# The last recurrent head of a hybrid layer takes two block sizes per step instead of one

## The chip, the cores and the metric

The kernel runs on one core of a Trainium2 chip. The metric is the device time of one execution in microseconds (us); for each kernel the median of several runs is given. A core has a matrix engine (PE, with its weight loads shown as PEld), a vector engine (DVE), a scalar engine (ACT), a general engine (POOL) and a sync engine (SP) that starts most transfers. Each works through its own list of instructions in order and waits for the others on semaphores. So a late instruction on one engine delays everything that stands behind it there, whether that needs the late data or not.

## The reference, cut to what matters

One layer of a model with 1024 tokens and width 1024, all in float32: a norm, one combined projection, then dilated attention (8 heads of 64) beside a gated linear recurrence (4 heads of 128), a projection of both, and a feed-forward part of width 4096. The change touches the recurrence alone. Within a chunk of 64 tokens it computes

```
diff = b[:, :, :, None, :] - b[:, :, None, :, :]      # b: running sum of the log gates
decay = jnp.exp(jnp.where(causal, diff, -jnp.inf))
a = jnp.einsum('bhtk,bhsk,bhtsk->bhts', qc, kc, decay)
o = o_inter + jnp.einsum('bhts,bhsv->bhtv', a, vc)
```

Here `a[t, s]` is the weight that token t gives to an earlier token s, with the product of all gates between them in it, separately for each of the 128 channels.

## The kernel before, in words

A float32 matmul of full precision is made here of three passes over high and low parts (`three_pass`, L91 to L93); a **group** below is three matmuls of 128x512, one for each pass. A weight tile comes by DMA, ACT rounds it to its high part (`wh`, L87) and DVE subtracts for the low part (`wl`, L88).

The recurrence uses chunks of 128 tokens, and `at` holds the weights `a` of all eight chunks. They are built up by block size. For blocks of c tokens, the queries of each second block and the keys of each first block are multiplied by their own gates inside the block (kept in `qt` and `kt`), a matmul gives all products of the two, a predicated copy under a mask writes those that belong to this size into `at`, and then `qt`, `kt` and the block totals `tot` are brought to size 2c. The diagonal comes from two sums over the channels (`pd`, L514), that go through a multiplication with the identity.

`hgrn_core` does this in two ways. Heads 0 to 2 climb two sizes per **step** (c to 4c, three steps, L542 to L574). Each 128x128 tile of keys is used as two halves of 64 columns, so that the array holds two chunk halves side by side, and the queries are first gathered into three sets of 32 columns by `quarter_sets` (L476; two ACT copies and two DVE products for each half of the tokens). A step is 16 matmuls of 64-column halves by 96 columns in two banks; behind it DVE runs products for `qt`, `kt` and `tot`, the products of the next `quarter_sets`, and six predicated copies. One last matmul of 64x64 blocks (L585) makes the size that is left. Head 3 instead takes one size per **level**, seven levels (L601 to L624): eight matmuls of 128x64 (L608; the trace counts each of these float32 matmuls twice), and on DVE a product for `kt` (L612), one for `qt` (L614), one for `tot` (L618) and one predicated copy under `masks` (L619).

Between steps and levels `fill(ns)` (L196) lets PE do other work: it pulls pieces from generators in `queue` until the given nominal time is used up, and what is overdrawn is carried on as a debt. A piece is mostly one group, counted as 650 ns. For heads 0 to 2 the pieces belong to the next recurrent head's projections. For head 3 they are `attn_proj` (L799), the projections of attention's first head pairs: queries in two halves (`pm_aq`, read by DVE into `qf`, L820, and split by ACT into `hiq`, L747, and by POOL, L748), values half 0 (`pm_av`, into `vf`, L837), keys half 0 and 1 (`pm_ak`, into `kf`, L754), values half 1. In the fourth piece of keys half 0 stand the transposes of `vf` (`values_turn`, L783, matmul L787, into the bank `pvt`). Generators that are not used up here are pulled on by the attention's steps later, the last of them at about 450 us.

Just ahead of head 3's core stands an exponential of one column (L1326), whose only purpose is to have ACT load its table of functions. The order of the instructions on each engine is that in which the code is written; buffers of the same name rotate.

Of the kernel before, what the change touches and what calls it, by code (L numbers as in the profile page):

```python
# [8 lines left out]
F32 = mybir.dt.float32  # L9
# [8 lines left out]
P = 128  # L18
# [19 lines left out]
def hymba_layer(ctx, tc, x, w_in, w_out, w_ff1, w_ff2, g_pre, lb_logits, g_mix, g_post,  # L38
# [28 lines left out]
    masks = cp.tile([P, len(LEVELS), 64], U8, name="masks")  # L67
# [313 lines left out]
    V.tensor_copy(masks, mraw)  # L381
# [123 lines left out]
    def hgrn_core(h, scale, after=None):  # L505
        hd = heads[h]
        inat, gate, prod, qt, kt, tot = (hd[n] for n in ("inat", "gate", "prod", "qt", "kt", "tot"))
        ready = quarter_sets(hd, h, 0, tot) if h < HH - 1 else None
        fill((5900 if 0 < h < HH - 1 else 5200) * scale)
        at = slab("S", f"at{h}", F32, (P, NT, P))  # L510
        for hf in range(2):
            pd = bank("pv", f"pd{h}_{hf}")
            for q in range(2):
                TE.matmul(pd, ones.to_broadcast([P, P]), prod[q][:, hf * 512:hf * 512 + 512], start=q == 0, stop=q == 1)  # L514
            pdv = pd.rearrange("p (n c) -> p n c", n=4)
            if h == HH - 1:
                V.tensor_tensor(out=at[:, hf * 4:hf * 4 + 4], in0=ident.unsqueeze(1).to_broadcast([P, 4, P]),
                                in1=pdv, op=ALU.mult)
                continue
            for a, b in halves:  # L520
                V.tensor_tensor(out=at[a:b, hf * 4:hf * 4 + 4, :64],
                                in0=ident[a:b, a:b].unsqueeze(1).to_broadcast([64, 4, 64]),
                                in1=pdv[a:b, :, a:b], op=ALU.mult)
# [5 lines left out]
        if h < HH - 1:  # L529
            fill(1200 * scale)  # L530
            totals = slab("P", f"tot{h}")
            for step in range(3):
                c = 4 ** step
                nb = 32 // c
                sets, cv = ready
                got = []
                for u in range(2):
                    pl = bank(("s", "t", "pv")[step], f"pl{h}_{step}{u}").rearrange("p (n q) -> p n q", n=4)
                    for n in range(4):
                        qs = sets[u][:, n].rearrange("p (s w) -> p s w", s=3)  # L540
                        for g, (a, b) in enumerate(halves):
                            TE.matmul(pl[a:b, n, :96], kt[:, (4 * u + n) * P + a:(4 * u + n) * P + b],  # L542
                                      qs[:, :, 32 * g:32 * g + 32], start=True, stop=True, skip_group_check=True)
                    got.append(pl)
                w = T // (4 * c)
                at_ = (0, 768, 960)[step]
                tots = totals[:, at_:at_ + 3 * w].rearrange("p (i w) -> p i w", i=3)
                u23, u123, nx = (tots[:, i] for i in range(3))
                cw = cv.rearrange("p n b f -> p (n b) f")
                q4 = qt.rearrange("p (m f c) -> p m f c", f=4, c=c)  # L550
                k4 = kt.rearrange("p (m f c) -> p m f c", f=4, c=c)

                def spread(ap, k=c):
                    return ap.unsqueeze(2).to_broadcast([P, w, k])
                V.tensor_tensor(out=q4[:, :, 1], in0=q4[:, :, 1], in1=spread(cw[:, :, 0]), op=ALU.mult)
                for hf in range(2):
                    n4 = slice(hf * 4, hf * 4 + 4)
                    V.tensor_tensor(out=qt[:, hf * 512:hf * 512 + 512].rearrange("p (n b f c) -> p n b (f c)", n=4, f=4, c=c)
                                    [:, :, :, 2 * c:],
                                    in0=sets[hf][:, :, 128:].rearrange("p n (b w) -> p n b w", b=nb),  # L560
                                    in1=cv[:, n4, :, 0:1].to_broadcast([P, 4, nb, 2 * c]), op=ALU.mult)
                V.tensor_tensor(out=u23, in0=cw[:, :, 2], in1=cw[:, :, 3], op=ALU.mult)
                V.tensor_tensor(out=u123, in0=cw[:, :, 1], in1=u23, op=ALU.mult)
                V.tensor_tensor(out=nx, in0=cw[:, :, 0], in1=u123, op=ALU.mult)
                if step < 2:
                    ready = quarter_sets(hd, h, step + 1, nx)
                V.tensor_tensor(out=k4[:, :, 2], in0=k4[:, :, 2], in1=spread(cw[:, :, 3]), op=ALU.mult)
                V.tensor_tensor(out=k4[:, :, 1], in0=k4[:, :, 1], in1=spread(u23), op=ALU.mult)
                V.tensor_tensor(out=k4[:, :, 0], in0=k4[:, :, 0], in1=spread(u123), op=ALU.mult)
                for u, pl in enumerate(got):  # L570
                    for part_, mask, c2 in ((0, own[:, 2 * step], c), (2, own[:, 2 * step + 1], 2 * c),
                                            (1, near[:, step], 2 * c)):
                        av = at[:, 4 * u:4 * u + 4, :64].rearrange("p n (b two c) -> p n b two c", two=2, c=c2)
                        V.copy_predicated(  # L574
                            av[:, :, :, 1, :],
                            mask.rearrange("p (b c) -> p b c", c=c2).unsqueeze(1).to_broadcast([P, 4, 32 // c2, c2]),
                            pl[:, :, part_ * 32:part_ * 32 + 32].rearrange("p n (b c) -> p n b c", c=c2))
                cur = nx
                table_part()
                fill(3500 * scale)  # L580
                table_part()
                fill(3500 * scale)
            pl = bank("s", f"pl{h}_6")
            for n in range(NT):
                TE.matmul(pl[:64, n * 64:(n + 1) * 64], kt[:, n * P:n * P + 64], qt[:, n * P + 64:(n + 1) * P],  # L585
                          start=True, stop=True)
            S.activation(at[64:, :, 64:], at[64:, :, :64], AF.Copy)
            G.memset(at[64:, :, :64], 0.0)
            S.activation(at[:64, :, 64:], pl[:64].rearrange("p (n c) -> p n c", n=NT), AF.Copy)
            kv, qv = (x.rearrange("p (n two c) -> p n two c", two=2, c=64) for x in (kt, qt))  # L590
            cv = cur.rearrange("p (n two) -> p n two", two=2)
            V.tensor_tensor(out=qv[:, :, 1], in0=qv[:, :, 1], in1=cv[:, :, 0:1].to_broadcast([P, NT, 64]), op=ALU.mult)
            V.tensor_tensor(out=kv[:, :, 0], in0=kv[:, :, 0], in1=cv[:, :, 1:2].to_broadcast([P, NT, 64]), op=ALU.mult)
            nx = tp.tile([P, NT], F32, tag="tot8", name=f"tot{h}_8", bufs=1)
            V.tensor_tensor(out=nx, in0=cv[:, :, 0], in1=cv[:, :, 1], op=ALU.mult)
            cur = nx
            fill(3400 * scale)
        else:
            cur = tot
            fill(1200 * scale)  # L600
            for li, c in enumerate(LEVELS):  # L601
                nb = 64 // c
                qv = qt.rearrange("p (b two c) -> p b two c", two=2, c=c)
                kv = kt.rearrange("p (b two c) -> p b two c", two=2, c=c)
                av = at.rearrange("p n (b two c) -> p n b two c", two=2, c=c)
                pl = bank("s", f"pl{h}_{li}")
                for n in range(NT):
                    TE.matmul(pl[:, n * 64:(n + 1) * 64], kt[:, n * P:(n + 1) * P],  # L608
                              qv[:, n * nb:(n + 1) * nb, 1, :], start=True, stop=True)
                w = T // (2 * c)  # L610
                cv = cur[:, :2 * w].rearrange("p (b two) -> p b two", two=2)
                V.tensor_tensor(out=kv[:, :, 0, :], in0=kv[:, :, 0, :],  # L612
                                in1=cv[:, :, 1:2].to_broadcast([P, w, c]), op=ALU.mult)
                V.tensor_tensor(out=qv[:, :, 1, :], in0=qv[:, :, 1, :],  # L614
                                in1=cv[:, :, 0:1].to_broadcast([P, w, c]), op=ALU.mult)
                nx = slab("P", f"tot{h}_{w}") if w > 32 else \
                    tp.tile([P, w], F32, tag=f"tot{w}", name=f"tot{h}_{w}", bufs=1)
                V.tensor_tensor(out=nx[:, :w], in0=cv[:, :, 0], in1=cv[:, :, 1], op=ALU.mult)  # L618
                V.copy_predicated(  # L619
                    av[:, :, :, 1, :],  # L620
                    masks[:, li].rearrange("p (b c) -> p b c", c=c).unsqueeze(1).to_broadcast([P, NT, nb, c]),
                    pl.rearrange("p (n b c) -> p n b c", n=NT, c=c))
                cur = nx
                fill((3700 if li == 0 else 2900 if li < 3 else 2200) * scale)  # L624
# [1701 lines left out]
```

## Time and profile before

| | us |
|---|---|
| three runs, median (lowest, highest) | 1198.26 (1198.24, 1198.39) |
| the profiled execution, its own time | 1197.81 |
| its span in the trace | 1195.6 |
| PE busy | 1186.2 (99% of the span) |
| DVE / ACT / POOL busy | 838.1 / 543.9 / 295.8 |

The profile is of one execution. Its page gives busy times and the chain of work that ended last; other views are the timeline (start, duration, engine, line, operation, output from inputs, how many alike in a row; in brackets the idle time ahead on that engine and what ended it), and windows (busy time per stretch, the granted clock of PE as a share of full speed, the share of DMA). Matmuls overlap, so that the time one takes from PE is read from start to start, not from its duration. Head 3's core lies at about 234 to 290 us.

### The profile page before, as it was taken

Reading aid. Unit: us, or ns where it says so; the run is one execution under the profiler, and the core shown is the slowest. Engines: PE = TensorE matmul, PEld = TensorE weight load, DVE = VectorE, ACT = ScalarE, POOL = GpSimd, SP = SyncE. Lnnn points to the kernel's source line nnn. Section 1 sums busy time; section 2 is a strip of 40 time slices with the busy share of each in tenths; the row PEclk is TensorE's granted clock in tenths of the full one; section 3 lists DMA queues with packets and bytes.
Section 4 is the critical chain, followed back from the end, with each engine's and each line's share of the span. In section 5 each row is a group of like instructions: output and inputs, shape, how many; then the busy total and the mean of one; then the engine's idle time right before and its main releaser. Section 6 shows DMA issues by size and latency. Waiting matters only on the chain.

```text
span 1195.6 us, 17551 instructions
## 1 busy us (share of the span) xinstructions
PE 1186.2 (99%) x6486; PEld 1014.5 (85%) x6486; DVE 838.1 (70%) x1393; ACT 543.9 (45%) x1068; POOL 295.8 (25%) x283
## 2 busy tenths in 40 slices
PE   9999999999999999999999999999999999999997
PEld 8898989888888888888888888888888888888886
DVE  5686969576666667675697666776687653578796
ACT  7633424322556667755653222222244544444562
POOL 0122222011111110152502777566540000000022
PEclk9999999999999999999999999999999999999999
DMA  5222323145454645362424465553687434533337
GB/s 220 71 68 85 98 84 98 52 119 144 125 133 104 153 135 143 96 233 96 169 97 161 174 215 207 179 183 142 218 325 273 159 105 143 174 89 105 106 106 282
DMA packets 90548, 175.48 MB, mean 147 GB/s; under 512 B 14944, under 2 KB 42464, under 8 KB 90464
## 3 DMA queue, kind: packets, MB, share of 16 engines
q1 hardware_dynamic: 90320, 174.37, 44.9%
q8 instruction: 51, 0.84, 0.3%
q14 instruction: 33, 0.27, 0.1%
q10 hardware_dynamic: 144, 0.00, 0.0%
HBM read 116.91 MB, written 47.99 MB: 138 GB/s over the span
## 4 chain that ended last, share of the span: by engine, by line
PE 96%; ACT 2%; DVE 1%; DMA 1%; issue 1%; POOL 0%; DVEq 0%; POOLq 0%; ACTq 0%
PE f L2066 18%; PE f2s L2066 7%; PE pig L91 3%; PE pig L93 2%; PE pig L92 2%; PE pwo L93 2%; PE pwo L91 2%; PE pwo L92 2%; PE pm_aq L91 1%; PE pm_f L91 1%; PE pm_ak L91 1%; PE pm_aq L93 1%; PE pm_aq L92 1%; PE pm_f L93 1%; PE pm_f L92 1%; PE pm_ak L93 1%
## 5 line engine op out<-in xcount | busy, mean ns | idle before, releaser
L88 DVE TENSOR_TENSOR al<-ar,ah 128x1024 fp32r<-128x1024 f32 x56 | 70.6, 1261 | 80.2 <-ACT ah L87 77.9
L2066 PE MATMUL f<-bh,ah 128*128 128x512 f32 x320 | 124.5, 389 | 0.0
L2066 PE MATMUL f<-bl,ah 128*128 128x512 f32 x320 | 124.5, 389 | 0.0
L2066 PE MATMUL f<-bh,al 128*128 128x512 f32 x320 | 124.5, 389 | 0.0
L87 ACT ACTIVATE ah<-ar 128x1024 fp32r<-128x1024 f32 x56 | 59.2, 1056 | 87.2 <-DMA ar<-actd 86.8
L2066 PEld LDWEIGHTS f<-bh,al 128*128 128x128 f32 x320 | 60.1, 188 | 12.6
L2066 PEld LDWEIGHTS f<-bl,ah 128*128 128x128 f32 x320 | 60.1, 188 | 12.5
L2066 PEld LDWEIGHTS f<-bh,ah 128*128 128x128 f32 x320 | 60.1, 188 | 12.3
L2140 POOL TENSOR_SCALAR lbl<-ssq 128x1 f32<-128x1 f32 x4 | 3.3, 821 | 245.7 <-ACT fd L2136 245.6
L1689 POOL TENSOR_TENSOR e<-x,e 128x512 f32<-128x512 f32 x14 | 21.6, 1540 | 130.1 <-DVE x L1640 123.0
L2066 PE MATMUL f2s<-bl,ah 128*128 128x512 f32 (+1 forms) x128 | 48.9, 382 | 0.0
L2066 PE MATMUL f2s<-bh,al 128*128 128x512 f32 (+1 forms) x128 | 48.9, 382 | 0.0
L2066 PE MATMUL f2s<-bh,ah 128*128 128x512 f32 (+1 forms) x128 | 48.9, 382 | 0.0
L732 POOL TENSOR_SCALAR tout<-traw 128x256 f32<-128x256 f32 x16 | 18.8, 1176 | 101.2 <-DMA traw<-in_bias_tab_dram 101.2
L88 DVE TENSOR_TENSOR bl<-br,bh 128x1024 fp32r<-128x1024 f32 x32 | 40.1, 1253 | 1.1 <-ACT bh L87 1.0
L2083 ACT ACTIVATE acc<-f 128x512 f32<-128x512 f32 x28 | 16.7, 597 | 48.6 <-PE f L2066 48.6
L87 ACT ACTIVATE bh<-br 128x1024 fp32r<-128x1024 f32 x32 | 33.6, 1051 | 4.3 <-PE f L2066 2.9
L88 DVE TENSOR_TENSOR wl<-raw,wh 128x1024 fp32r<-128x1024 f32 x21 | 25.9, 1234 | 10.2 <-ACT wh L87 10.2
L778 POOL TENSOR_TENSOR kl<-kf,kh 64x512 fp32r<-64x512 f32 x12 | 15.4, 1287 | 69.5 <-ACT kh L777 48.0
L91 PE MATMUL pwo<-woh,mt 128*128 128x512 f32 x80 | 32.2, 402 | 0.0
L93 PE MATMUL pwo<-woh,mt 128*128 128x512 f32 x80 | 31.3, 391 | 0.0
L92 PE MATMUL pwo<-wol,mt 128*128 128x512 f32 x80 | 31.2, 390 | 0.0
(1728 smaller groups left out, 3901.4 us busy)
## 6 DMA issues: line engine op xcount, KB each, us to landing
ar<-actd SPq DMA_DIRECT2D x56, 512.0 KB, 3.6
br<-in_w_ff_dram SPq DMA_DIRECT2D x16, 1024.0 KB, 5.8
raw<-in_w_in_dram SPq DMA_DIRECT2D x28, 512.0 KB, 4.2
w1r<-in_w_ff_dram SPq DMA_DIRECT2D x14, 1024.0 KB, 6.4
actd<-e SPq DMA_DIRECT2D x17, 768.0 KB, 4.3
actd<-e SPq DMA_DIRECT2D x11, 1024.0 KB, 4.1
xr<-in_x_dram SPq DMA_DIRECT2D x8, 512.0 KB, 8.2
raw<-in_w_out_dram SPq DMA_DIRECT2D x8, 512.0 KB, 3.6
```

Source lines behind the costliest of these rows:

```text
L87: S.activation(hi, src, AF.Copy)
L88: eng.tensor_tensor(out=lo, in0=src, in1=f32(hi), op=ALU.subtract)
L91: TE.matmul(dst, lhs[0], rhs[0], start=start, stop=False)
L92: TE.matmul(dst, lhs[0], rhs[1], start=False, stop=False)
L93: TE.matmul(dst, lhs[1], rhs[0], start=False, stop=stop)
L732: G.tensor_scalar(by_class(dst[:, part_ * w:(part_ + 1) * w]), in_blocks(raw[:, FAR * DIL:]), 8.0, None, op0=ALU.mult)
L778: G.tensor_tensor(out=kl[a:b], in0=src, in1=f32(kh[a:b]), op=ALU.subtract)
L1689: eng[0].tensor_tensor(out=e1[:, 3], in0=a21, in1=e1[:, 2], op=ALU.add)
L2066: TE.matmul(pm, a[:, j, c], b[:, j, d], start=start and j == 0 and q == 0, stop=stop and j == 1 and q == 2, skip_group_check=True)
L2083: S.activation(acc_at(p, i), pm, AF.Copy)
L2140: G.tensor_scalar(base[:, t:t + 1], sums[j][:, t:t + 1], 1.0 / D, EPS, op0=ALU.mult, op1=ALU.add)
```

## The change

Head 3 now runs the same three steps and the 64x64 matmul as the others. Its levels are gone from the code, and with them the tile `masks` and the cast that filled it (L381). The fillings in head 3 were scaled by 1.15 and are now scaled by 1.0; the first, ahead of `pd`, goes from 5980 to 5200 ns nominal, and that is from ten groups to eight. All line numbers of the changed kernel are lower, by 2 at L80 and by 34 at the end.

```diff
-    masks = cp.tile([P, len(LEVELS), 64], U8, name="masks")
...
-    V.tensor_copy(masks, mraw)
...
     def hgrn_core(h, scale, after=None):
         hd = heads[h]
         inat, gate, prod, qt, kt, tot = (hd[n] for n in ("inat", "gate", "prod", "qt", "kt", "tot"))
-        ready = quarter_sets(hd, h, 0, tot) if h < HH - 1 else None
+        ready = quarter_sets(hd, h, 0, tot)
         fill((5900 if 0 < h < HH - 1 else 5200) * scale)
...
-            if h == HH - 1:
-                V.tensor_tensor(out=at[:, hf * 4:hf * 4 + 4], in0=ident.unsqueeze(1).to_broadcast([P, 4, P]),
-                                in1=pdv, op=ALU.mult)
-                continue
             for a, b in halves:
                 V.tensor_tensor(out=at[a:b, hf * 4:hf * 4 + 4, :64],
                                 in0=ident[a:b, a:b].unsqueeze(1).to_broadcast([64, 4, 64]),
                                 in1=pdv[a:b, :, a:b], op=ALU.mult)
...
-        if h < HH - 1:
-            fill(1200 * scale)
-            totals = slab("P", f"tot{h}")
-            for step in range(3):
...
-            cur = nx
-            fill(3400 * scale)
-        else:
-            cur = tot
-            fill(1200 * scale)
-            for li, c in enumerate(LEVELS):
...
-                fill((3700 if li == 0 else 2900 if li < 3 else 2200) * scale)
+        fill(1200 * scale)
+        totals = slab("P", f"tot{h}")
+        for step in range(3):
...
+        cur = nx
+        fill(3400 * scale)
...
-        last_gate = hgrn_core(h, 1.15 if last else 1.0, open_attention if last else None)
+        last_gate = hgrn_core(h, 1.0, open_attention if last else None)
```

Three places show how the instructions now stand. A row is the line, the operation, the output with its buffer number, the inputs, and the shape.

The first is ACT at the start of head 3's core. Before:

```order
L463 ACTIVATE prh3_2602<-pr31_2735 128x512
L1326 ACT_TABLE_LOAD
L1326 ACTIVATE texp_2740<-nhalf_86 128x1
L87 ACTIVATE wh17_2758<-raw17_2513 128x1024
L473 ACTIVATE rc1_2767<-rrow_128 128x512
L474 ACTIVATE rrow_128<-rc1_2767 128x512
L747 ACTIVATE hiq00_2780<-qf00_2778 128x512
```

and in the change:

```order
L461 ACTIVATE prh3_2600<-pr31_2733 128x512
L1292 ACT_TABLE_LOAD
L1292 ACTIVATE texp_2738<-nhalf_85 128x1
L485 ACTIVATE qs3_00_2740<-qt3_2513 128x4x64
L489 ACTIVATE qs3_00_2740<-qt3_2513 128x4x32
L485 ACTIVATE qs3_01_2745<-qt3_2513 128x4x64
L489 ACTIVATE qs3_01_2745<-qt3_2513 128x4x32
L86 ACTIVATE wh17_2766<-raw17_2511 128x1024
L471 ACTIVATE rc1_2775<-rrow_127 128x512
L472 ACTIVATE rrow_127<-rc1_2775 128x512
L713 ACTIVATE hiq00_2788<-qf00_2786 128x512
```

The four gathering copies stand between the table load and the next weight's rounding, and so ahead of all that follows on ACT.

The second is DVE around the read of the values, `vf`. Before:

```order
L619 COPY_PREDICATED at3_2794<-masks_78,pl3_1_2854 128x256x2
L88 TENSOR_TENSOR wl18_2878<-raw18_2623,wh18_2877 128x1024
L612 TENSOR_TENSOR kt3_2604<-kt3_2604,tot3_256_2865 128x128x4
L614 TENSOR_TENSOR qt3_2515<-qt3_2515,tot3_256_2865 128x128x4
L618 TENSOR_TENSOR tot3_128_2900<-tot3_256_2865 128x128
L619 COPY_PREDICATED at3_2794<-masks_78,pl3_2_2889 128x128x4
L837 TENSOR_TENSOR vf00_2906<-pm_av00_2847,rrow_128 128x512
L791 TENSOR_TENSOR v0_2846<-pvt00_2925,v0_2846 128x8x64
```

and in the change:

```order
L560 TENSOR_TENSOR kt3_2602<-kt3_2602,tot3_2815 128x64x4
L561 TENSOR_TENSOR kt3_2602<-kt3_2602,tot3_2815 128x64x4
L562 TENSOR_TENSOR kt3_2602<-kt3_2602,tot3_2815 128x64x4
L567 COPY_PREDICATED at3_2795<-own_78,pl3_10_2909 128x4x8x4
L567 COPY_PREDICATED at3_2795<-own_78,pl3_10_2909 128x4x4x8
L567 COPY_PREDICATED at3_2795<-near_79,pl3_10_2909 128x4x4x8
L567 COPY_PREDICATED at3_2795<-own_78,pl3_11_2918 128x4x8x4
L567 COPY_PREDICATED at3_2795<-own_78,pl3_11_2918 128x4x4x8
L567 COPY_PREDICATED at3_2795<-near_79,pl3_11_2918 128x4x4x8
L803 TENSOR_TENSOR vf00_2961<-pm_av00_2887,rrow_127 128x512
L757 TENSOR_TENSOR v0_2886<-pvt00_2980,v0_2886 128x8x64
```

The read of the values stood behind the third level and stands now behind the whole second step (`pl3_10` and `pl3_11` are its two banks).

The third is PE around the transposes of `vf`. Before:

```order
L91 MATMUL pm_ak00_2912<-hTh00_90,wh18_2877 128x512
L92 MATMUL pm_ak00_2912<-hTl00_91,wh18_2877 128x512
L93 MATMUL pm_ak00_2912<-hTh00_90,wl18_2878 128x512
L787 MATMUL pvt00_2925<-ident_77,vf00_2906 128x128 x4
L608 MATMUL pl3_3_2936<-qt3_2515,kt3_2604 128x64 x8
L91 MATMUL pm_ak00_2912<-hTh10_92,wh18_2877 128x512
```

and in the change:

```order
L90 MATMUL pm_ak00_2967<-hTh00_89,wh18_2903 128x512
L91 MATMUL pm_ak00_2967<-hTl00_90,wh18_2903 128x512
L92 MATMUL pm_ak00_2967<-hTh00_89,wl18_2904 128x512
L753 MATMUL pvt00_2980<-ident_77,vf00_2961 128x128 x4
L90 MATMUL pm_ak00_2967<-hTh10_91,wh18_2903 128x512
L91 MATMUL pm_ak00_2967<-hTl10_92,wh18_2903 128x512
```

The transposes keep their place among the groups; three levels lay ahead of them and two steps do now, and the level that followed them at once is gone.

More of the change, by code (lines that the diff above doesn't have):

```diff
@@ L528, in hgrn_core @@
             load_bias(0)
-        if h < HH - 1:
-            fill(1200 * scale)
-            totals = slab("P", f"tot{h}")
-            for step in range(3):
[L533 to L577, printed above, removed]
-                cur = nx
[L579 to L595, printed above, removed]
-            cur = nx
-            fill(3400 * scale)
-        else:
-            cur = tot
-            fill(1200 * scale)
-            for li, c in enumerate(LEVELS):
[L602 to L623, printed above, removed]
-                fill((3700 if li == 0 else 2900 if li < 3 else 2200) * scale)
@@ new lines, in hgrn_core @@
+        pl = bank("s", f"pl{h}_6")
+        for n in range(NT):
+            TE.matmul(pl[:64, n * 64:(n + 1) * 64], kt[:, n * P:n * P + 64], qt[:, n * P + 64:(n + 1) * P],
+                      start=True, stop=True)
+        S.activation(at[64:, :, 64:], at[64:, :, :64], AF.Copy)
+        G.memset(at[64:, :, :64], 0.0)
+        S.activation(at[:64, :, 64:], pl[:64].rearrange("p (n c) -> p n c", n=NT), AF.Copy)
+        kv, qv = (x.rearrange("p (n two c) -> p n two c", two=2, c=64) for x in (kt, qt))
@@ L625, in hgrn_core @@
+        cv = cur.rearrange("p (n two) -> p n two", two=2)
+        V.tensor_tensor(out=qv[:, :, 1], in0=qv[:, :, 1], in1=cv[:, :, 0:1].to_broadcast([P, NT, 64]), op=ALU.mult)
+        V.tensor_tensor(out=kv[:, :, 0], in0=kv[:, :, 0], in1=cv[:, :, 1:2].to_broadcast([P, NT, 64]), op=ALU.mult)
+        nx = tp.tile([P, NT], F32, tag="tot8", name=f"tot{h}_8", bufs=1)
+        V.tensor_tensor(out=nx, in0=cv[:, :, 0], in1=cv[:, :, 1], op=ALU.mult)
+        cur = nx
+        fill(3400 * scale)
         ktr = slab("T", f"ktr{h}", F32, (P, NT, P))
```

48 lines of the change are left out of this document (added).

## The prediction

> **What bounds the kernel now.** I read the page first, for which engine sets the end, then windows for the stretch that the change touches.
>
> ```profile
> PE 1186.2 (99%) x6486; PEld 1014.5 (85%) x6486; DVE 838.1 (70%) x1393; ACT 543.9 (45%) x1068; POOL 295.8 (25%) x283
> PE 96%; ACT 2%; DVE 1%; DMA 1%; issue 1%; POOL 0%; DVEq 0%; POOLq 0%; ACTq 0%
> 240.00:300.00 60.00, 60.00 (x361) 1.00 0.49 133
> ```
>
> The second row is the chain that ended last: PE holds 96% of it. The third is a window of PE alone, from 240 to 300 us: 60.00 of 60 us busy, at a granted clock of 1.00. So every matmul that leaves this stretch is worth its whole time, and every wait put into it costs its whole time, because nothing idles there now. DVE's 70% is a mean over the program and says little here; what decides is whether DVE, working through its list in order, brings each thing before PE asks for it.
>
> **The matmuls that go.** Their time from PE is read in the timeline (start and duration first), between the starts of neighbours that stay.
>
> ```profile
> 249.83 1.89 PE L608 MATMUL pl<-qt,kt 128*128 128x64 f32 x16
> 255.06 1.89 PE L608 MATMUL pl<-qt,kt 128*128 128x64 f32 x16
> ...
> 269.79 1.89 PE L608 MATMUL pl<-qt,kt 128*128 128x64 f32 x16
> 274.34 1.89 PE L608 MATMUL pl<-qt,kt 128*128 128x64 f32 x16
> ...
> 185.66 1.54 PE L542 MATMUL pl<-qs,kt 128*64 128x96 f32 x32
> 194.88 1.54 PE L542 MATMUL pl<-qs,kt 128*64 128x96 f32 x32
> ...
> 70.82 0.28 PE L93 MATMUL pig<-wig1h,hTl 128*128 128x256 f32 x1
> 78.01 0.28 PE L93 MATMUL pig<-wig1h,hTl 128*128 128x256 f32 x1
> ...
> 213.00 0.39 PE L93 MATMUL pm_q<-hTh,wl 128*128 128x512 f32 x1
> 213.31 1.15 PE L585 MATMUL pl<-qt,kt 128*64 128x64 f32 x16
> 214.72 0.39 PE L92 MATMUL pm_q<-hTl,wh 128*128 128x512 f32 x1
> ```
>
> Between the first two levels lie five groups in 5.23 us, between the next two four groups in 4.55. The difference, 0.68, is a group, and a level is 4.55 − 4 × 0.68 = 1.83. Seven make 12.81. The two steps of head 2 are 9.22 apart with 63 matmuls of 128x256 between; 60 spacings of those take 78.01 − 70.82 = 7.19, or 0.12 each. A step is 9.22 − 63 × 0.12 = 1.67, three are 5.01. The 64x64 matmuls sit between 213.00 and 214.72 with two spacings of 0.227 (a third of a group) beside them: 1.72 − 0.45 = 1.27. So PE is relieved of 12.81 − 5.01 − 1.27 = **6.53 us**. These are spacings of the same shapes at a clock of 1.00, so I give this term hardly any error.
>
> **The cast of the masks.** The timeline at the start of the program, DVE and then PE:
>
> ```profile
> 44.63 0.39 DVE L381 CAST masks<-mraw 128x448 uint8<-128x448 f32 x1
> 44.94 0.34 DVE L383 TENSOR_REDUCE lowhalf<-mraw 128x3 f32<-128x192 f32 x1
> ...
> 49.78 0.50 PE L91 MATMUL pm_f<-hTh,wh 128*128 128x512 f32 x1 [0.54 <-DVE qt L441]
> ```
>
> Without it all that stands behind it on DVE comes 44.94 − 44.63 = 0.31 sooner. At 49.78 PE waited 0.54 for DVE, and that product stands behind the masks in DVE's list. I take **−0.31**; if something slower on ACT feeds the wait it is 0. Nothing makes it a loss.
>
> **The filling.** The scale of 1.0 removes no work: a group not pulled here is pulled later. It moves `pd` two groups, 1.36 us, ahead, and the totals of the fillings are such that head 3 pulls two groups more in all, which are then missing in attention at about 450 us.
>
> **What DVE now has to do before the transposes.** This is the term that decides. `vf`, which the transposes need, stands behind the whole second step on DVE, so I follow DVE from the table load until there. Rows of the timeline of head 2 (180 to 204 us) price the step, rows of head 3 (from 241 us) all the rest.
>
> ```profile
> 182.70 0.42 ACT L487 ACTIVATE qs<-qt 128x256 f32<-128x256 f32 x1
> 184.00 1.04 ACT L87 ACTIVATE wh<-raw 128x1024 fp32r<-128x1024 f32 x1
> ...
> 186.25 1.71 DVE L521 TENSOR_TENSOR at<-ident,pd 64x256 f32<-64x256 f32 x4
> 187.97 0.64 DVE L555 TENSOR_TENSOR qt<-qt,tot 128x256 f32<-128x256 f32 x1
> 193.17 1.08 DVE L568 TENSOR_TENSOR kt<-kt,tot 128x256 f32<-128x256 f32 x1
> 194.10 0.63 DVE L569 TENSOR_TENSOR kt<-kt,tot 128x256 f32<-128x256 f32 x1
> 197.22 0.45 DVE L555 TENSOR_TENSOR qt<-qt,tot 128x256 f32<-128x256 f32 x1
> 203.68 0.90 DVE L555 TENSOR_TENSOR qt<-qt,tot 128x256 f32<-128x256 f32 x1
> ...
> 241.43 1.28 ACT L1326 ACT_TABLE_LOAD   x1
> 242.83 1.04 ACT L87 ACTIVATE wh<-raw 128x1024 fp32r<-128x1024 f32 x1
> ...
> 243.91 1.23 DVE L88 TENSOR_TENSOR wl<-raw,wh 128x1024 fp32r<-128x1024 f32 x1 [1.77 <-ACT wh L87]
> 245.05 0.68 DVE L820 TENSOR_TENSOR qf<-pm_aq,rrow 128x512 f32<-128x512 f32 x1
> 245.65 1.27 DVE L517 TENSOR_TENSOR at<-ident,pd 128x512 f32<-128x512 f32 x2
> 250.90 0.69 DVE L820 TENSOR_TENSOR qf<-pm_aq,rrow 128x512 f32<-128x512 f32 x1
> 251.62 0.63 ACT L747 ACTIVATE hiq<-qf 128x512 fp32r<-128x512 f32 x1 [5.16 <-DVE qf L820]
> 252.16 1.04 ACT L87 ACTIVATE wh<-raw 128x1024 fp32r<-128x1024 f32 x1
> ...
> 260.27 0.60 PE L787 MATMUL pvt<-ident,vf 128*128 128x128 f32 x4
> ```
>
> One: head 2 itself has no slack. Its first step's last `kt` product begins at 194.10 and ends at 194.73, and PE takes up the second step at 194.88. A DVE that starts a step later there makes PE wait.
>
> Two: the start. Before, ACT rounds the weight at 242.83, behind the table load. Four gathering copies (182.70 to 184.00, so 1.30) now come ahead: 244.13. DVE's `wl` follows 243.91 − 242.83 = 1.08 behind, at 245.21. Then 1.14 to `qf` and 0.60 to `at`, which in the four small pieces of head 2 takes 187.97 − 186.25 = 1.72: the first step begins at 245.21 + 1.14 + 0.60 + 1.72 = 248.67.
>
> Three: the first step takes 197.22 − 187.97 = 9.25 (no wait of DVE stands in that stretch), to 257.92. Then the second `qf`; its `hiq` starts 0.72 behind it, the next `wh` 0.54 behind that, and `wl` 1.08 later, as in the rows above: 257.92 + 2.34 = 260.26, and 1.14 more to 261.40.
>
> Four: the second step takes 203.68 − 197.22 = 6.46, to 267.86; `vf` is a read of the same form as `qf`, 0.69 long: the transposes can start at about 268.6. PE would want them at 260.27 − 3 × 1.83 + 2 × 1.67 = 258.12, with the same groups ahead and two steps in place of three levels. **PE loses 268.6 − 258.1 = 10.5 us** up to here, in pieces: at `pd` (`prl` comes no sooner, and `pd` is wanted 1.36 sooner), at the second step's matmuls, at the first group of keys half 0 (its `wh` stands behind the second `qf`), and the largest, some 4 to 5 us, at the transposes. Behind the transposes only one step and the 64x64 matmul are left, DVE's third step is the shortest, and the levels that kept it busy there are gone; I see nothing late, so 0 more.
>
> **Bounds of this term.** The 1.08 at 193.17 is against 0.63 for the same form at 194.10: 0.45 that head 2 met there and head 3 need not. Low: 10.0. For the high end, two rows of head 3's timeline:
>
> ```profile
> 246.54 1.30 POOL L748 TENSOR_TENSOR qf<-qf,hiq 128x512 fp32r<-128x512 f32 x1 [11.03 <-ACT hiq L747]
> 246.84 1.54 DVE L612 TENSOR_TENSOR kt<-kt,tot 128x512 f32<-128x512 f32 x1
> 251.76 0.69 DVE L612 TENSOR_TENSOR kt<-kt,tot 128x512 f32<-128x512 f32 x1 [0.17 <-PE pl L608]
> ```
>
> While POOL made a low part, a DVE product took 1.54 in place of 0.69. Two such splits fall into the two steps; at 0.85 each the term is 12.2. The Trainium skill says the same in its page "SBUF — State Buffer", section "Who interferes with whom": a vector operation with two inputs from SBUF and a GpSimd operation lock each other out. The trace agrees, 1.54 against 0.69.
>
> **The end of the filling.**
>
> ```profile
> 452.12 0.40 PE L91 MATMUL pwe<-woh,emt 128*128 128x512 f32 x1
> 455.47 0.39 PE L915 MATMUL ps_N<-kh,q 128*128 128x256 f32 x1 [0.20 <-DVE stat L920]
> ```
>
> At about 450 two groups vanish, just ahead of the product with `emt`, whose factors come from DVE and ACT. A wait on DVE's `stat` stands three us later already, so this stretch has little slack; between 0 (all slack) and 1.36 (none) I take **+0.8**. The two groups themselves are paid for in head 3, so their own time cancels; only the waits that come in their place are a loss.
>
> **Sum.** −6.53 − 0.31 + 10.5 + 0.8 = +4.5. The profiled execution took 1197.81; 1202.3. The median of the runs, 1198.26, stands 0.45 above it, so the forecast is about **1202.8 us**. Its own range: low −6.53 − 0.31 + 10.0 + 0 = +3.2, high −6.53 + 0 + 12.2 + 1.36 = +7.0, which is 1201.4 to 1205.3.
>
> **Rivals.**
>
> *The matmuls' saving lands in full.* For it speaks that PE is at 60.00 of 60 and that DVE idled 1 to 2 us behind several levels. Against it stands the chain above: `vf` would have to be ready 10 us before its own engine gets to it. It would give 1198.26 − 6.84 = 1191.4, faster. I give it 0.06.
>
> *Half covered.* DVE's steps are shorter than in head 2, where other engines' work delayed it, or PE's waits overlap with something I count twice. It needs a chain shorter by 2 to 6 us: within ±2.4 us of before, about 1199.5. That is 0.13. (0.2%, or 2.4 us, is about what a measurement of this kernel can tell from no change.)
>
> *The clock falls as well.* One wait of 4 to 5 us at the transposes might cost PE its clock.
>
> ```profile
> 1180.00:1196.00 16.00, 9.58 (x65) 0.86 0.76 291
> ```
>
> In the last 16 us PE works 9.58, up to about 1189.6, and the granted clock's mean is 0.86. If it is 0.5 when it falls, it lay there for 0.14 × 16 / 0.5 = 4.5 us, from about 1191.5, so 1.9 us after the last matmul. A wait of 4.7 us is longer than that. At half clock each us of matmuls costs one more; a fall that lasts through two to five groups behind the wait (1.4 to 3.4 us of work) costs 1.4 to 3.4, and the time is about 1205. From when it decides: a single wait over some 2 us. The shorter pieces of the 10.5 would not do it. No row shows how soon the clock returns; I give it 0.25. The Trainium skill's page "TensorE: Matmul & The Clock Gate", Part 1, section "The HAM clock gate", has the clock halved after an idle window of about 3.4 us and given back after as long a busy one; by it the price would be an estimate of 3.4 us.
>
> **Chances.** Forecast 0.56, clock 0.25, half covered 0.13, saved in full 0.06. The likeliest number is 1202.8; faster than 0.2% is 0.06 and a little of the half covered case, 0.08 in all; within 0.2% 0.13; slower 0.79. The range takes the half covered case in its upper part and the clock case whole: 1199.8 to 1206.5.
>
> **What would show it.** Right: waits of PE in the window from 240 to 275, at `pd` for `prl`, at the second step for `kt`, at keys half 0 for `wh` or `wl`, and over 4 us at `pvt` for `vf`, together about 10; three groups of 32 matmuls in place of seven of 16. The chain of waits would leave PE for DVE there. Wrong: PE without gaps in that window, DVE's first step under 8 us, the transposes at 258, or a wait behind them that I left out. For the clock: a window behind the transposes below 1.00.

## The result: slower, by twice what was forecast

The changed kernel takes 1207.96 us (median of four runs, 1207.43 to 1209.69) against 1198.25 for the kernel before: a ratio of 1.0084, 95% interval 1.0066 to 1.0101. That is 9.7 us more. The forecast was 4.5 us more, with a range that ended at 1206.5: the direction was right, the size was not.

The profiled execution of the change took 1209.69 us (span 1207.9), the slowest of the four, and 11.9 us more than that of before (1197.81). The ledger below is made between these two traces. First the page and windows of PE alone (length, busy time with the number of matmuls, granted clock, share of DMA, GB/s) of the change:

```profile
PE 1186.9 (98%) x6486; PEld 1008.7 (84%) x6486; DVE 838.9 (69%) x1426; ACT 548.4 (45%) x1082; POOL 296.9 (25%) x284
...
PE 89%; DVE 5%; ACT 3%; issue 1%; DMA 1%; SPq 0%; POOL 0%; DVEq 0%; POOLq 0%; ACTq 0%
...
240.00:280.00 40.00, 31.37 (x202) 0.96 0.30 82
280.00:320.00 40.00, 37.90 (x217) 0.96 0.60 146
```

PE's part of the chain fell from 96% to 89%, and DVE's rose from 1% to 5%. Where PE had been busy for 60 of 60 us, it is now idle for 8.6 of the first 40 and 2.1 of the next, and the granted clock is below 1.00 in both. What PE waited for there (the view of waits, 230 to 310 us: total, times, longest):

```profile
PE pvt L753 <- DVE vf L803: 4.2, 1, 4.2
PE pl L535 <- DVE kt L562: 1.8, 1, 1.8
PE pm_aq L90 <- ACT wh L86: 1.5, 1, 1.5
PE pm_ak L90 <- ACT wh L86: 0.9, 1, 0.9
PE pm_ak L92 <- DVE wl L87: 0.8, 1, 0.8
PE pd L512 <- ACT prh L461: 0.7, 1, 0.7
PE pm_aq L92 <- DVE wl L87: 0.5, 1, 0.5
PE pd L512 <- DVE prl L463: 0.2, 1, 0.2
```

Six of the eight are the waits of the forecast, in the places it named (at `pd` most of it, 0.7 us, was for `prh` from ACT, where the forecast had only `prl`). The two of `pm_aq` (the queries of the second head pair, 2.0 us in all) it did not have. The timeline of the change has the chain on DVE and the transposes on PE:

```profile
247.11 1.71 DVE L515 TENSOR_TENSOR at<-ident,pd 64x256 f32<-64x256 f32 x4
248.83 0.95 DVE L548 TENSOR_TENSOR qt<-qt,tot 128x256 f32<-128x256 f32 x1
...
254.80 0.60 DVE L562 TENSOR_TENSOR kt<-kt,tot 128x256 f32<-128x256 f32 x1
...
257.88 0.71 DVE L786 TENSOR_TENSOR qf<-pm_aq,rrow 128x512 f32<-128x512 f32 x1
...
261.61 0.41 DVE L548 TENSOR_TENSOR qt<-qt,tot 128x256 f32<-128x256 f32 x1
...
267.76 0.69 DVE L803 TENSOR_TENSOR vf<-pm_av,rrow 128x512 f32<-128x512 f32 x1
...
268.51 1.11 PE L753 MATMUL pvt<-ident,vf 128*128 128x128 f32 x4 [4.22 <-DVE vf L803]
```

The first step begins on DVE at 248.83 (forecast 248.67), ends at 257.88 (257.92), the second begins at 261.61 (261.40), `vf` at 267.76 (267.86) and the transposes at 268.51 (268.6). Priced from rows of another head, the points of this chain were right to 0.2 us. Two pieces were off by more, and offset each other: the turn with the second `qf` and the weight took 3.73 us in place of 3.48, the second step 6.15 in place of 6.46.

The clock stands in windows of 3.41 us, laid so that their edges fall on its changes:

```profile
264.65:268.06 3.41, 0.00 (x0) 1.00 0.26 105
268.06:271.47 3.41, 2.96 (x9) 0.50 0.00 0
271.47:274.88 3.41, 3.41 (x41) 1.00 0.60 154
...
288.54:291.95 3.41, 1.56 (x6) 1.00 0.82 184
291.95:295.36 3.41, 3.41 (x11) 0.50 0.90 201
295.36:298.77 3.41, 3.41 (x25) 1.00 0.34 114
```

It fell to half twice, for one such window each: once behind the wait at the transposes, and once, unforeseen, behind the two waits of `pm_aq`. With 2.96 and 3.41 us of work in the halved windows, that costs half of each: 1.5 + 1.7 = 3.2 us.

How much later the same matmul starts than before, at four points of the program:

| matmul | before, us | later in the change by | forecast |
|---|---|---|---|
| last group of `pm_f`, ahead of head 3 | 234.50 | 0.16 | −0.31 |
| first transposes `pvt` | 260.27 | 8.24 | 8.0 |
| first scores of attention, `ps_D` | 292.65 | 11.21 | 5.0 |
| first matmul of the feed-forward part, `f` | 884.47 | 12.01 | 4.5 |

(The forecast column adds its terms in order: −0.31; then −3 × 1.83 + 2 × 1.67 + 10.5; then −4 × 1.83 + 1.67 + 1.27 and the two groups more, 1.36; then −1.36 + 0.8.) The forecast holds as far as the transposes. Behind them 6 us come in addition: 3.2 from the clock, 2.4 from the two waits of `pm_aq` (2.05 of idle time and 0.17 more at each restart, since matmuls normally overlap by that much), 0.4 unassigned. And between 293 and 884 us come 0.8 in place of −0.56.

### The profile page after: what moved, and what is told of

It is laid out like the page before. It is cut to its first block, busy times and chain, and to the rows that moved or that the text cites. A ratio compares the mean times of both kernels' runs of the same rounds, so it can differ in the third digit from the quotient of the medians.

```text
span 1207.9 us, 17596 instructions
## 1 busy us (share of the span) xinstructions
PE 1186.9 (98%) x6486; PEld 1008.7 (84%) x6486; DVE 838.9 (69%) x1426; ACT 548.4 (45%) x1082; POOL 296.9 (25%) x284
## 4 chain that ended last, share of the span: by engine, by line
PE 89%; DVE 5%; ACT 3%; issue 1%; DMA 1%; SPq 0%; POOL 0%; DVEq 0%; POOLq 0%; ACTq 0%
PE f L2032 18%; PE f2s L2032 7%; PE pig L90 2%; PE pig L92 2%; PE pig L91 2%; PE pwo L90 2%; PE pwo L92 2%; PE pwo L91 2%; PE pl L535 1%; PE pm_aq L92 1%; PE pm_ak L90 1%; PE pm_q L90 1%; PE pm_aq L90 1%; PE pm_ak L91 1%; PE pm_ak L92 1%
```

## The experiments

The theory after the result: DVE's list is the cause of the first part, and three things that follow from its lateness are the rest, namely the keys' path behind the transposes, the clock, and attention's lack of cover. The first rival is the filling: the scale of 1.0 might do the harm, not the steps.

**The levels with a scale of 1.0.** The kernel before, with one number changed:

```diff
-        last_gate = hgrn_core(h, 1.15 if last else 1.0, open_attention if last else None)
+        last_gate = hgrn_core(h, 1.0, open_attention if last else None)
```

> The kernel before (seven levels) with nothing but the filling of head 3 at a scale of 1.0. Theory (the lateness of the vector engine behind the steps is what costs): the diagonal's matmuls come two groups sooner and wait 0.9 us as they do in the change, the levels behind them stay covered, some wait comes in attention where groups are now missing or left over: 1199 to 1201 us, and no fall of the clock. Rival (the smaller filling is what makes work late): at least half of the 9.7 us shows here, 1203 us or more.

Measured 1213.14 us, ratio 1.0122 (1.0105 to 1.0139): slower than the change itself. My theory of 1199 to 1201 missed by 12 us. The waits of PE between 235 and 520 us:

```profile
PE ps_N L915 <- DMA kh<-kh: 3.0, 1, 3.0
PE ps_N L916 <- DMA kl<-kl: 1.3, 3, 0.9
PE ps_F L915 <- DVE stat L920: 1.1, 2, 0.6
PE pt_F L995 <- ACT pf L973: 1.0, 1, 1.0
...
PE pd L514 <- ACT prh L463: 0.7, 1, 0.7
```

In head 3 only the diagonal waits, 0.7 and a little, as it should. The loss comes later: the first scores start 2.8 us earlier than before, the feed-forward part 15.0 later. Ahead of the first scores, counted from the end of `pm_f`, stand 49 groups here, 55 before and 57 in the change. What is not projected in head 3 has to be projected inside attention, which then waits for transfers of keys (`kh<-kh`, `kl<-kl`); and the clock, for which the theory had no fall, was halved for two windows of 3.41 us there (from 404.12). So the amount of filling in head 3 is not free, which the prediction had assumed ("a group not pulled here is pulled later"). But this loss is not that of the change: with its steps, a scale of 1.0 pulls two groups more than before, not six fewer, and it lost 11.2 of its 12.0 us ahead of the scores, where the levels with a scale of 1.0 lost none.

**The steps with a scale of 1.15.** The change with the number put back.

> The change with the filling of head 3 left at 1.15. Rival (the smaller filling is what costs): with it back, waits go and the saving of 6.5 us shows: 1200 us or less. Theory (the vector engine's list is as long as before): 24 groups now lie ahead of the second step, so the values are read ahead of that step's block and the wait of 4.2 us at their transposes goes, but the vector engine ends both blocks no sooner, and a like wait comes at the next things read behind them (the keys); with 9 groups more pulled in head 3 attention lacks cover. 1205 to 1212 us.

Measured 1213.1 us, ratio 1.0124 (1.0106 to 1.0142), 1 us above the theory's bound, 13 above the rival's. The wait at the first transposes is gone, as 24 groups put the read of the values ahead of the second step, and PE waits instead for the weight of the keys (3.2 us), behind the first transposes (1.6) and for statistics in attention (3.9). The clock was halved three times for two windows each (from 259.50, 310.70 and 464.30). Neither amount of filling rescues or explains the steps: with the levels 1.15 was right, with the steps 1.0 pulls about as much in all.

**The transposes eight groups later.**

```diff
-                if n == 3 and hf == 0:
+                if n == 3 and hf == (1 if pr == 0 else 0):
                     values_turn()
```

> The change, with the transposes of the first values moved from the fourth group of keys half 0 to the fourth group of keys half 1, eight groups or 5.4 us later. Theory: the wait of 4.2 us there was lateness of one read on the vector engine, and the fall of the clock at its end hangs on it: both go, 4.2 + 1.7 us, 1207.9 - 5.9 = about 1202; up to 2 more if the wait for the weight behind the second keys (2.0 us) shrinks too. Rival (the lateness is passed on to the keys and the weight behind them): 1206 us or more. Rival on the clock: the wait goes and the clock falls all the same, 1203.7.

Measured 1202.81 us, ratio 1.0035 (1.0022 to 1.0048); the theory said about 1202. The wait at the transposes is gone, and with it one of the two falls; the other (from 284.37, behind a wait for the same weight of 1.6 + 0.5) is still there. This one wait and its fall were worth 5.2 us of the 9.7.

**Waits of six sizes.** The kernel before, with products that change nothing ahead of the key products in heads 0 to 2:

```diff
+                for _ in range({(0, 0): 2, (0, 1): 10, (1, 0): 4, (1, 1): 8, (2, 0): 6, (2, 1): 12}.get((h, step), 0)):
+                    V.tensor_tensor(out=qt[:, :512], in0=qt[:, :512], in1=qt[:, :512], op=ALU.max)
```

> The kernel before with 2 to 12 extra products of 128x512 on the vector engine (each the larger of a value and itself, so nothing changes) ahead of the key products of steps in heads 0 to 2, to make the matrix engine wait there for about 1, 2, 3, 4, 5 and 6 us, each more than 8 us from the next. Theory on the clock (it is granted in stretches of 3.41 us and falls to half for one stretch when the matrix engine idled for over about half of the stretch before): waits under 1.5 us bring no fall, waits over 3.5 us always one, between them it depends on where the stretch begins; each fall costs 1.7 us beside the wait. Rival (a fall needs a wait of a whole 3.41 us): none for waits under 3.4 us.

The one execution took 1229.1 us. PE waited 0.70, 5.67, 2.21, 4.34, 4.72 and 5.47 us; the clock fell behind the last three and the second, not behind 0.70 and 2.21. Two falls and the wait without one, again in windows of 3.41 us:

```profile
142.17:145.58 3.41, 2.98 (x25) 1.00 0.15 41
145.58:148.99 3.41, 1.63 (x33) 1.00 0.07 19
...
155.82:159.23 3.41, 0.83 (x7) 1.00 0.05 17
159.23:162.64 3.41, 1.66 (x21) 0.50 0.58 176
162.64:166.06 3.42, 3.42 (x22) 0.50 0.19 52
...
213.84:217.25 3.41, 0.34 (x8) 1.00 0.35 120
217.25:220.66 3.41, 3.41 (x36) 0.50 0.27 79
220.66:224.08 3.42, 3.42 (x30) 1.00 0.26 75
```

The four falls begin at 90.96, 159.23, 217.25 and 230.91: 20, 17 and 4 windows of 3.41 apart, so they sit on one grid. A window with 0.83 us of work is followed by a halved one, and one with 1.66 of work at half clock by a second; a full window ends it. None of the waits was between 2.2 and 3.4 us, but the change itself decides against the rival: its second fall followed waits of 1.5 and 0.5 us, neither near 3.41. The Trainium skill ("TensorE: Matmul & The Clock Gate", Part 1, "The HAM clock gate") names an idle window of about 3.4 us for the fall and a busy one of that length for the return. The trace agrees on the length; it differs in that the window need not be idle. On the grids of all the traces here, from 40 to 1186 us, every window at full clock with less than 1.6 us of work in 3.41 was followed by a halved one, and none with more than 2.2. Between these the busy time does not decide: falls came behind 1.75 us (256.79 to 260.20 in the run with the table load later) and 2.20 (460.88 to 464.30 in the steps with a scale of 1.15), none behind 1.63 (above) and 2.05 (280.68 to 284.09 in the run with four moves).

**The weight behind the second keys.** The change, with the split called before the keys are read:

```diff
+            if pr == 0 and hf == 1:
+                w_get(A0 + 2)
             keys_read(pr, box[0], hf)
```

> The change, with the split of the next queries' weight (the one waited for at 289.86, 2.0 us in two pieces) called before the second keys are read, so that on the scalar engine it no longer stands behind the second keys' high part, which waits there 8.5 us for a transfer. Theory: the two waits go, and the second fall of the clock, which begins at the end of a stretch with these two waits in it, goes with them: 2.0 + 1.7 less, 1204 to 1205. Rival (the lateness moves on to the next thing read on the vector engine, the second values): 1206 us or more.

Measured 1207.64 us, ratio 1.0079 (1.0064 to 1.0094): the rival. The two waits of `pm_aq` are gone, and the transposes of the second values wait in their place:

```profile
PE pvt L753 <- DVE vf L803: 6.2, 2, 4.2
PE pl L535 <- DVE kt L562: 1.8, 1, 1.8
```

Two waits of `vf`, 4.2 and 2.0. The second fall of the clock is gone in the profiled execution all the same (one is left, from 268.32), which is 2.1 us shorter than that of the change; the medians differ by 0.3. So the weight was not the cause of the lateness there but the first to show it. Its cause stands in the waits of DVE and ACT of the change (255 to 310 us):

```profile
DVE kf L720 <- DMA kh<-hik: 7.0, 1, 7.0
...
DVE vf L803 <- DMA kh<-hik: 1.2, 1, 1.2
...
ACT hik L713 <- DMA kl<-kf: 8.5, 1, 8.5
```

The keys, their high part and the values pass through two small buffers (`half`, L61), and each is free for the next only when its transfers have landed. DVE waited 7.0 us to read the second keys and ACT 8.5 to make their high part, with the weight queued behind. Before, the levels' matmuls covered this round of transfers. These are the two reads of keys before, and then in the change:

```profile
265.47 0.69 DVE L754 TENSOR_TENSOR kf<-pm_ak,rrow 128x512 f32<-128x512 f32 x1 [0.78 <-PE pm_ak L93]
274.60 0.69 DVE L754 TENSOR_TENSOR kf<-pm_ak,rrow 128x512 f32<-128x512 f32 x1 [0.86 <-issue]
...
276.88 0.68 DVE L720 TENSOR_TENSOR kf<-pm_ak,rrow 128x512 f32<-128x512 f32 x1
284.60 0.69 DVE L720 TENSOR_TENSOR kf<-pm_ak,rrow 128x512 f32<-128x512 f32 x1 [7.03 <-DMA kh<-hik]
```

Before, PE itself took 9.1 us from the last matmul of the first keys to that of the second (265.04 to 274.12), with two levels between, and DVE waited for no transfer. In the change it took 5.5 us (274.59 to 280.05), less than the 7.7 between the two reads. The levels are what the change removed. No run put other work in their place, so that they were the cover is read from these times, not tried.

**The table load later.** The change, with the exponential moved behind the first filling:

```diff
+        if h == HH - 1:
+            S.activation(col("texp"), nhalf[:, :1], AF.Exp)
```

> The change, with the table load and its exponential moved behind the first filling, so that on the scalar engine the gathering copies, the next weight's high part and the rearrangement of the row factors come first. Theory (the vector engine's list is one chain from that weight on): all of it comes 1.3 to 1.4 us sooner, 1206.5 or so. Rival (the chain is set by the diagonal's sums and not by the table load): no change, 1208 us.

Measured 1207.23 us, ratio 1.0074 (1.0059 to 1.0089): between theory and rival, which at this distance the medians do not part. The traces do: the first transposes start 6.59 us later than before in place of 8.24 and their wait is 2.6 us in place of 4.2. The table load was on the chain, and 1.6 us of it came free; by the medians 0.7 of that reached the end. PE came to the transposes no sooner (264.2 us, as in the change): it waited 1.2 us less at the second step, but the first of two falls of the clock lay ahead of the transposes here, from 260.20.

**Four moves together.** The table load, the transposes, the next queries' weight as above, and the keys' weight split ahead of the read of the second queries:

```diff
+            if pr == 0 and hf == 1:
+                w_get(A0 + 1)
             full = half(f"qf{pr}{hf}", F32R)
```

> The change with four things moved: the table load behind the first filling, the transposes of the first values into keys half 1, the split of the keys' weight ahead of the read of the second queries, and that of the next queries' weight ahead of the read of the second keys. Theory: the waits of 4.2, 1.8, 0.9 + 0.8 and 2.0 us shrink to about 3 in all with the 0.9 at the diagonal, no fall of the clock: 1207.9 - 7.9 - 3.4 = about 1196.5. Rival (the vector engine has too much to do for these stages, whatever the order): 1200 us or more.

Measured 1204.23 us, ratio 1.005 (1.0033 to 1.0067): the rival's side, and worse than moving the transposes alone. The waits of PE in it (235 to 520 us):

```profile
PE pvt L755 <- DVE vf L807: 5.3, 1, 5.3
...
PE pl L537 <- DVE kt L564: 0.7, 1, 0.7
PE pd L514 <- ACT prh L461: 0.7, 1, 0.7
```

Every wait of the list is small but one: the second transposes, 5.3 us, with a fall of the clock behind it.

**The copies late.** As the four moves, and in head 3 the predicated copies are issued between the two halves of the step's filling:

```diff
+            if h < HH - 1:
+                own_blocks()
...
-            fill(3500 * scale)
+            fill(((4200, 3500, 2900)[step] if h == HH - 1 else 3500) * scale)
             table_part()
-            fill(3500 * scale)
+            if h == HH - 1:
+                own_blocks()
+            fill(((4200, 2850, 2850)[step] if h == HH - 1 else 3500) * scale)
```

> As the kernel with four moves, and in head 3 the six predicated copies of each step are issued behind the first half of the filling that follows the step, with fillings of 4200 + 4200, 3500 + 2850 and 2900 + 2850. Theory: only the wait of 0.9 us at the diagonal is left, 1.4 us better than the four moves alone: about 1195, faster than both kernels. Rival (the copies then delay the next step's products as much): as the four moves or slower.

Measured 1200.31 us, ratio 1.0018 (1.0008 to 1.0027): 3.9 better than the four moves, yet 5 above the theory. The run moves the filling as well as the copies, and the two are not parted. DVE is no longer late for the steps; the second transposes still wait 3.1 us with a fall behind them. The timeline tells why:

```profile
265.00 0.68 DVE L727 TENSOR_TENSOR kf<-pm_ak,rrow 128x512 f32<-128x512 f32 x1
...
268.66 0.63 ACT L720 ACTIVATE hik<-kf 128x512 fp32r<-128x512 f32 x1 [8.45 <-PE pvt L760]
...
277.60 0.63 ACT L720 ACTIVATE hik<-kf 128x512 fp32r<-128x512 f32 x1 [5.39 <-DMA kl<-kf]
...
285.63 0.69 DVE L812 TENSOR_TENSOR vf<-pm_av,rrow 128x512 f32<-128x512 f32 x1 [9.85 <-DMA kh<-hik]
...
286.38 0.92 PE L760 MATMUL pvt<-ident,vf 128*128 128x128 f32 x4 [3.11 <-DVE vf L812]
```

With the transposes moved eight groups back, the first values hold one of the two small buffers until 268. So the first keys, read at 265.00, got their high part only at 268.66, 3.7 later; then each turn of the two buffers takes 8 to 9 us (268.66, 277.60, 285.63).

**The transposes in the seventh group of keys half 0.** As the last, with `n == 6` in half 0 for the first pair.

> As the kernel with the late copies, but the transposes of the first values stand in the seventh group of keys half 0 in place of the fourth of keys half 1. There the values' buffer was held until 268 us, the high part of the first keys (which needs it) came 3.7 us after the keys, and so the second values, which need the buffers of both keys' halves, came 3.1 us late. Theory (the two rounds of key transfers through two small buffers are the next limit): the high part now follows the keys within 1 us, the wait of 3.1 us at the second transposes falls below 1, the fall of the clock goes with it: 1200.3 - 2.3 - 1.7 = about 1196.5. Rival (that wait has another cause): 1199 us or more.

Measured 1196.75 us, ratio 0.9985 (0.9975 to 0.9994); the theory said 1196.5. The high part now follows the first keys within 0.8 us, but the wait that was to fall below 1 us is still 1.4. No fall of the clock is left up to the last matmuls, and the longest waits are

```profile
PE pvt L760 <- DVE vf L812: 1.4, 1, 1.4
PE ps_D L892 <- DVE stat L897: 0.8, 1, 0.8
PE pd L514 <- ACT prh L461: 0.7, 1, 0.7
PE pov L1008 <- DVE stat L936: 0.5, 1, 0.5
```

**The high parts from another queue.** As that, and

```diff
-                    nc.sync.dma_start(out=dst[c:d], in_=f32(src[a:b]).rearrange("p (r m) -> p r m", r=DIL))
+                    (nc.scalar if q == "kh" else nc.sync).dma_start(out=dst[c:d], in_=f32(src[a:b]).rearrange("p (r m) -> p r m", r=DIL))
```

> As that kernel, and the four transfers of the keys' high parts are started by the scalar engine in place of the sync engine, so that the eight transfers of a half no longer start one behind another 0.65 us apart. Theory (the starting of transfers makes each round 8 to 9 us long): the second keys and the second values come 2 us sooner, and what is left of the wait goes: 0 to 1 us faster than with all on the sync engine. Rival (the scalar engine loses more by starting them): slower than that kernel by 1 us or more.

Measured 1196.47 us, ratio 0.9983 (0.9974 to 0.9993). The 0.3 us between the two lie inside their intervals, and the waits of 0.5 us and more are the same: whether starting the transfers matters is not shown. This is the fastest kernel of the study, 1.9 us under the kernel before and 11.5 under the change.

**Four of the moves with the levels.** The kernel before with the table load, both weights and the queue moved; the transposes, the copies and the filling stay as they were.

> The kernel before, with its seven levels and its scale of 1.15, and those moves of the fastest version that it can take: the table load behind the first filling, the two weights split earlier, the keys' high parts started by the scalar engine. Theory (the matrix engine waits for nothing in this stretch with the levels, so moves give nothing; what the fastest version gains is the steps' 6.5 us, less what waits are left): no change, 1198.3 within 0.7. Rival (the moves are worth something by themselves, and the steps nothing): 1196.5 or so.

Measured 1198.17 us, ratio 0.9998 (0.9988 to 1.0008): no change, the theory. These four moves give nothing by themselves. The other place of the transposes and the smaller filling were not tried with the levels; but PE waits for nothing between `pm_f` and the first scores before (58.15 of 58.15 us busy), so there is no wait there that they could take away. By this argument what the fastest version gains comes from the steps, and the moves only let a part of it through.

## Where the prediction held and where it failed

The direction, the saving and the chain up to the transposes held. The time came out above the range because the sum had nothing for two things behind the transposes, the clock (3.2 us measured) and the turns of the key buffers (2.4), and 1.4 us too little for the cover that attention lost.

- **6.53 us of matmuls saved: not contradicted.** The ledger closes with it to 0.4 us. The trace of the fastest version comes near it as well: from the end of `pm_f` to the first scores it takes 56.11 us in place of 58.15, with two groups more (1.36), 2.34 us of idle time and three restarts of 0.17; without these the difference is 6.2.
- **0.31 from the cast: not seen.** The wait at `pm_f` shrank to 0.2 us, but a wait of 0.3 came in at a step of head 2 and PE stood 0.16 late at 234.5. In the other runs without the cast the same matmul starts between 0.28 us earlier and 0.37 later than before, so a term of this size cannot be read from one trace.
- **10.5 us up to the transposes: right**, 10.2 by the table above (8.24 − 0.16 + 2.15), in the pieces named, the last of them 4.2 where 4 to 5 was written.
- **"I see nothing late, so 0 more" behind the transposes: the step that failed.** I followed DVE and asked of each matmul whether DVE was in time; I did not ask what the four levels behind the transposes had covered. They covered two rounds of key transfers through two buffers. It measured 2.4 us, first at a weight, and when that was cleared at the second transposes.
- **The clock: left out of the sum, a rival at 0.25, and it happened**, twice. My condition, "a single wait over some 2 us", was too narrow: 1.5 and 0.5 in one window sufficed. It cost 3.2 us in the profiled execution, 1.5 and 1.7 for a halved window of 3.41 us. The estimate of 3.4 for one fall was wrong in its own terms: at half clock such a window does 1.7 us of work and so costs 1.7. The other executions were 1.4 to 2.3 us shorter; their mean clocks (0.996, 0.997 and 0.998 against 0.997) do not show whether they had a fall less.
- **The end of the filling, +0.8 on a saving of 1.36: too small.** Between the scores and the feed-forward part the change loses 0.8 more, although two groups are missing there: 2.2 us of cover in place of 0.8. PE waits twice at `pt_F` (0.4 each) where the groups were; all its waits behind the first scores add up to 0.9 us more than before, and the rest is not located. The run with the levels and a scale of 1.0 shows how steep this is: with six groups moved from head 3 into attention it took 15 us more.

Together 2.4 + 0.4 + 3.2 + 1.4 are the 7.4 us by which the profiled execution exceeds the 4.5. What stays open is the attention part of it: the two fastest versions, too, give back 0.7 and 1.4 us between the first scores and the feed-forward part, and no experiment here looked into that.

## What to carry to other kernels

Matmuls that are removed from a stretch in which PE never waits were also the cover of every other engine's work there: for each one removed, ask not only whether its own successor comes in time, but how long the transfers and the turns of buffers are that now have less time. Follow the lateness past the first wait, since clearing one wait handed it on to the next three times here (a weight, the second transposes, a buffer), and only the removal of the last let the gain through. And price a wait of PE by the windows in which the clock is granted: here a window of 3.41 us at full clock with less than 1.6 us of work always brought a halved one, and a halved window cost half the work in it, up to 1.7 us.

## What the runs showed of the hardware

The granted clock changes only at the edges of a grid of 3.41 us that stays in phase over a run (falls 20, 17 and 4 windows apart). A window at full clock with under 1.6 us of work is followed by one at 0.50, and short waits in the same window add up (1.5 and 0.5 us sufficed); between 1.6 and 2.2 us of work it went either way. The clock returns after a halved window that was mostly busy: 2.90 us in the run with four moves and 2.96 in the change sufficed, 0.5 to 2.42 did not, and neither did 2.95 in attention (464.30 to 467.71 in the steps with a scale of 1.15). And six groups pulled later moved the time by 15 us, more than the change under study did.
